# Six edits to a hybrid decoder trunk in split float32: pinned memory scaling, squares on two engines, values out of the bank, weight sums, convolution root, one more tile

## The chip, the cores and the metric

The kernel runs on one core of a Trainium2 chip. The metric is device microseconds (us) of one launch; lower is better. TensorE is PE in all views, VectorE is DVE, ScalarE is ACT, GpSimd is POOL, and SP is the queue that issues most loads. Each engine works off its own instructions in order; engines wait for each other by semaphores.

## The reference

One layer (`DEPTH` 1) on x of 1024 x 1024, in float32. All products have K of 1024. Cut to what matters here:

```python
h = rms_norm(x, norm_g[l])
z = jnp.einsum('bsd,de->bse', h, w_in[l])          # 11 blocks of 1024 columns
u = jax.nn.gelu(z[..., OFF_A_U:OFF_A_U + W])
v = layer_norm(jax.nn.gelu(z[..., OFF_A_V:OFF_A_V + W]), gmlp_ln_g[l], gmlp_ln_b[l])
br_a = gmlp_spatial_gate(u, v, w_s[l], b_s[l]) * jax.nn.silu(z[..., OFF_A_G:OFF_A_G + W])
glu = z[..., OFF_B_A:OFF_B_A + W] * jax.nn.sigmoid(z[..., OFF_B_B:OFF_B_B + W])
c = causal_depthwise_conv(glu, conv_w[l], conv_b[l])            # 31 taps
c = jax.nn.silu(layer_norm(c, conv_ln_g[l], conv_ln_b[l]))
br_b = c * jax.nn.silu(z[..., OFF_B_G:OFF_B_G + W])
mem_n = rms_norm(mem, mem_norm_g[l])                            # 256 x 1024
att = memory_cross_attention(z[..., OFF_C_Q:OFF_C_Q + W], mem_n, w_kv[l])
br_c = att * jax.nn.silu(z[..., OFF_C_G:OFF_C_G + W])
proj = jnp.einsum('bsnw,nwd->bsnd', branches, w_branch[l])
merged = jnp.einsum('bsnd,bsnd->bsd', gates, proj)              # sigmoid gates out of z
x = x + jnp.einsum('bsd,de->bse', merged, w_out[l])
return rms_norm(x, final_norm_g)
```

## The kernel before

Every float32 operand is split into a high part (a cast to fp32r on ACT, L74, or a scaled copy) and a low part (the difference, on DVE, L75); a product is then three matmuls, high x high, high x low and low x high. Where the names end in `hi` and `lo`, or a tile has a leading index 0 and 1, these are the two parts. The large products use seven block products in place of eight; the sums of blocks are formed on DVE for x (`combine`) and, for two of the weights, on the way through DRAM.

The program runs in this order, with the times of the profiled execution:

- **K projection**, 0 to 39 us. `mem_gain(k)` (L210, L211) scales the memory's columns into `mhi`/`mlo`, eight K steps of 128x256 out of two loads `mraw`. Two groups `g` of four weight tiles `kraw`, each of two K steps; a tile goes through `wchunk` (cast `whi`, difference `wlo`), the first one in two halves; L269 does the matmuls. After the fourth tile come the squares of `mtok` (the memory by rows, L135, with a row sum) and `mean_rsqrt` (L99 to L109) for the norm; `diagonals` (L121) puts the result on the diagonal of tiles `dg`, and `spread` (L130, L132) multiplies them with ones, which gives the norm along the other axis.
- **V projection**, 39 to 63 us (L332). Beside it ACT squares the tiles `xtok` (x by rows, eight loads, three of them ahead, `NRAW`) by `squares(n)` into the columns of `xss`. A finished bank is scaled into `vt` (L345) and split from there into `vv`.
- **v of the gMLP**, 66 to 155 us (L380), 16 chunks of 24 matmuls. Behind the first chunk the program does `squares(3)`, `mean_rsqrt` and `diagonals` for x, and behind the second the spread into `rb`, which `x_norm` (L299) multiplies into x.
- **40 half pairs**, 156 to 950 us (L425): the other blocks of `w_in`, some 19 us each. Beside the matmuls DVE forms sums of weight tiles (`sum`, split into `op`), ACT copies one of the banks away (`u`, L462 and L469, for which PE's next block product waits), and DVE does the convolution's 31 taps in pieces (L523). Also here, by a generator `wsum`, the sums of tiles of the branch and output weights: a base load on SP (L629), up to three accumulating DMAs on POOL (L627), a cast `wsh` on ACT and the difference on DVE; both parts are stored later by `flush`. `spump(n)` takes n steps of the list of generators, `spump(1)` ahead of a half pair and `spump(SPUMP)` behind it.
- **Attention and merge**, 951 to 1190 us (L732, L770, L806). `conv_rstd` (L863) makes the reciprocal root of the convolution's mean square: `csq` holds squares, summed over channels tile by tile; a product with `onesd` (L845) sums over partitions, so that each of 128 partitions holds the same 1024 values, and the root is worked out on 128x1024 in two halves. `normed` (L882) multiplies it in. In this stage each bank leaves by `gate` (L739) on DVE.
- **Output product**, 1190 to 1344 us (L938): seven block products again, whose sums of blocks are `sums4` on DVE and whose parts are cast and subtracted as `op`.

The order on each engine follows a scheduler that starts from the program's order; it may move an instruction ahead of others on its engine where nothing depends on it. `keep(...)` around an instruction holds it in the written order.

Of the kernel before, what the change touches and what calls it, by code (L numbers as in the profile page):

```python
# [39 lines left out]
def trunk(ctx, tc, xt, x, memt, wf, wv, wkf, wkv, mem, wbr, wb1, wo, wst, bs, cols, fng, out):  # L40
# [92 lines left out]

    def square(src, dst):
        A.activation(out=src, in_=src, func=AF.Square, accum_out=dst)  # L135

# [29 lines left out]
    def c1(base, k):  # L166
        return col[:, base + k:base + k + 1]
# [40 lines left out]
    def mem_gain(k):  # L208
        src = mraw[k // 4][:, k % 4, :]
        A.activation(out=mhi[k], in_=src, func=AF.Copy, scale=c1(COL_MEMN, k))  # L210
        V.scalar_tensor_tensor(out=mlo[k], in0=src, scalar=c1(COL_MEMN, k), in1=f(mhi[k]),  # L211
                               op0=ALU.mult, op1=ALU.subtract)

# [35 lines left out]
    for g in range(2):  # L249
        pst = [bank() for _ in range(4)]  # L250
        for j in range(4):
            i = 4 * g + j
            if i == 0:
                hi, lo = op((P, 1024), "whi"), op((P, 1024), "wlo")
                for kk2 in range(2):
                    v = slice(kk2 * H, (kk2 + 1) * H)
                    split(kraw[0][:, v], hi[:, v], lo[:, v])
                    mem_gain(kk2)
            else:
                hi, lo = wchunk(None, kraw[i])  # L260
                if g == 0:
                    mem_gain(2 * j)
                    mem_gain(2 * j + 1)
# [47 lines left out]
    def squares(n):  # L311
        for _ in range(n):
            t = min(xtok)
            square(xtok.pop(t), xss[:, t:t + 1])
            if t + NRAW < TT:
                xt_load(t + NRAW)

    for hf in range(2):
        pst = [bank() for _ in range(MT)]
        for c in range(4):  # L320
# [16 lines left out]
            if i == 1:  # L337
                for t in range(NRAW):
# [28 lines left out]
    for th in range(2):  # L367
        va = [slot(s="va") for _ in range(4)]
        for ch in range(2):
            pst = [bank() for _ in range(4)]  # L370
            for c in range(4):
# [249 lines left out]

    def wsum(w, i, j):
        t = slot(F32R, s="ws")
        for n, b in enumerate((SUMB, SUMO)[w][i]):
            src = (wb1, wo)[w][b + j]
            if n:
                G.dma_start(out=f(t), in_=src, accum_op=ALU.add)  # L627
            else:
                nc.sync.dma_start(out=f(t), in_=src)  # L629
                flush()  # L630
            yield
        hi = slot(F32R, s="wsh")
        split(f(t), hi, t)
        unstored.extend(((sdram[w, i, j][0], f(hi)), (sdram[w, i, j][1], f(t))))
        yield

    sums = [wsum(w, i, j) for w in range(2) for i in SUMB for j in range(2)]

    def spump(n):
        while n and sums:  # L640
            try:
                next(sums[0])
                n -= 1
            except StopIteration:
                sums.pop(0)
                if not sums:
                    flush()

# [213 lines left out]
    def conv_rstd():  # L862
        nonlocal crs  # L863
        ps = flat(tokmean(wchunk(None, csq)))
        a, s, y = slot(s="ca"), slot(s="cs"), slot(s="crb")
        for hf in range(2):
            v = slice(hf * H, (hf + 1) * H)
            V.tensor_scalar(a[:, v], ps[:, v], LN_EPS, None, ALU.add)
            A.activation(out=s[:, v], in_=a[:, v], func=AF.Sqrt)
            V.reciprocal(out=y[:, v], in_=s[:, v])  # L870
            V.tensor_tensor(s[:, v], y[:, v], y[:, v], ALU.mult)
            V.tensor_tensor(s[:, v], s[:, v], a[:, v], ALU.mult)
            V.tensor_scalar(s[:, v], s[:, v], -0.5, 1.5, ALU.mult, ALU.add)
            V.tensor_tensor(y[:, v], y[:, v], s[:, v], ALU.mult)
        crs = y

# [10 lines left out]
    for d in range(KT):  # L887
# [200 lines left out]
    s1 = [slot(shape=(P, 2, H), s="s1") for _ in range(2)]  # L1088
    s1 = [s1[k // 2][:, k % 2, :] for k in range(4)]
    sums4(s1, a21, a22)  # L1090
# [20 lines left out]
    oprod(px, o, w, False)  # L1111
    sums4(a12, a12, a11, ALU.add)
    o, w = [gop(v) for v in a12], wn
# [11 lines left out]

SPUMP = 2
NVA = 2
# [11 lines left out]
PUMPA = 8  # L1139
NWARM = 10  # L1140
PUMP = (6, 4, 6, 3, 6, 8, 6, 6, 5, 7)

# [56 lines left out]
```

## Time and profile before

| | |
|---|---|
| runs, us | 1349.16, 1350.61, 1353.12; median 1350.61 |
| profiled execution, us | 1355.2, span 1353.5, mean granted clock 0.987 |
| busy, us | PE 1309.0, DVE 1101.8, ACT 610.9, POOL 117.2 |

A launch's time is a little longer than the span between the first and last instruction of its profile. "Busy" counts time in which an engine executes; weight loads of PE lie beside its matmuls. Idle time of an engine matters only where another one, in the end PE, waits for it.

### The profile page before, as it was taken

The page shows a single profiled execution, that of the slowest core. Times are in us where ns is not written, and L with a number is a line of the kernel's source. Part 1 is how long each engine was busy: PE and PEld are TensorE (multiplying, and loading weights), DVE is VectorE, ACT ScalarE, POOL GpSimd, SP SyncE. Part 2 cuts the span into 40 slices and gives each one's busy share as a digit, 9 for nine tenths or more (in the row PEclk, how much of TensorE's full clock was granted, in tenths as well). Part 3 has the DMA queues.
Part 4 walks back from the last instruction along what each step waited for, and adds up shares of the span by engine and source line. Part 5 has one row for each costly group of instructions (what it writes and reads, how often), then busy time and mean ns, then how long its engine had stood idle before and what let it go on. Part 6 is the DMA issues. An engine that isn't in the chain of part 4 may idle for free.

```text
span 1353.5 us, 16391 instructions
## 1 busy us (share of the span) xinstructions
PE 1309.0 (97%) x6006; PEld 1089.7 (81%) x6006; DVE 1101.8 (81%) x1479; ACT 610.9 (45%) x1017; POOL 117.2 (9%) x203
## 2 busy tenths in 40 slices
PE   7899999999899999999999999999999999799997
PEld 7788888888688788778888888888888888688785
DVE  4788768998885997998899898698599478984776
ACT  5856655344344444344344444344544453322235
POOL 0100011111110111110210000001000010000000
PEclk8999999999899999999999999999999999899998
DMA  9844366766666657556864313335744453656943
GB/s 368 349 141 156 119 232 186 209 205 194 226 194 148 250 193 242 187 173 197 229 217 171 102 63 109 124 141 203 259 169 133 171 218 109 246 189 239 406 177 125
DMA packets 84465, 262.86 MB, mean 194 GB/s; under 512 B 8608, under 2 KB 18336, under 8 KB 84384
## 3 DMA queue, kind: packets, MB, share of 16 engines
q1 hardware_dynamic: 56704, 161.83, 34.1%
q0 software_dynamic: 27392, 99.63, 22.7%
q8 instruction: 47, 0.77, 0.2%
q10 hardware_dynamic: 288, 0.35, 0.1%
q14 instruction: 34, 0.28, 0.1%
HBM read 185.23 MB, written 76.55 MB: 193 GB/s over the span
## 4 chain that ended last, share of the span: by engine, by line
PE 78%; DVE 10%; DMA 7%; issue 3%; ACT 2%; SPq 0%; POOL 0%; DVEq 0%; POOLq 0%; ACTq 0%
PE x L425 24%; PE y L425 12%; PE acc L938 11%; PE acc L732 11%; PE b L380 7%; PE z L425 6%; DMA ws<-in_wb 2%; DVE conv L523 2%; PE acc L770 2%; DVE op L75 2%; PE acc L806 2%; DMA ws<-in_wo 2%; DMA raw<-in_wf 1%; PE b L269 1%; PE b L332 1%
## 5 line engine op out<-in xcount | busy, mean ns | idle before, releaser
L425 PE MATMUL x<-T,op 128*128 128x512 f32 x1440 | 349.7, 392 | 8.8 <-ACT u L462 8.8
L425 PEld LDWEIGHTS x<-T,op 128*128 128x128 f32 x1440 | 270.8, 189 | 67.5 <-ACT u L462 11.4
L523 DVE SCALAR_TENSOR_TENSOR conv<-cb,col,conv 128x994 f32<-128x994 f32 (+14 forms) x120 | 151.8, 1265 | 0.6
L74 ACT CAST op<-sum 128x512 fp32r<-128x512 f32 x160 | 99.4, 622 | 104.7 <-PE z L425 40.1
L75 DVE TENSOR_TENSOR op<-sum,op 128x512 fp32r<-128x512 f32 x160 | 108.7, 685 | 18.8 <-ACT op L74 18.6
L425 PE MATMUL x<-B,op 128*128 128x512 f32 x480 | 115.9, 389 | 2.6 <-DVE op L75 2.6
L425 PE MATMUL z<-B,op 128*128 128x512 f32 x480 | 115.9, 390 | 1.0 <-DVE op L75 1.0
L425 PE MATMUL y<-B,op 128*128 128x512 f32 x480 | 115.4, 389 | 0.0
L425 PE MATMUL y<-T,op 128*128 128x512 f32 x480 | 115.3, 389 | 0.0
L523 DVE SCALAR_TENSOR_TENSOR conv<-ca,col,conv 128x994 f32<-128x994 f32 (+14 forms) x90 | 113.6, 1262 | 0.3
L425 PEld LDWEIGHTS x<-B,op 128*128 128x128 f32 x480 | 90.0, 188 | 21.7 <-DVE op L75 3.1
L425 PEld LDWEIGHTS z<-B,op 128*128 128x128 f32 x480 | 89.9, 188 | 20.5 <-DVE op L75 1.9
L425 PEld LDWEIGHTS y<-B,op 128*128 128x128 f32 x480 | 90.1, 188 | 18.7
L425 PEld LDWEIGHTS y<-T,op 128*128 128x128 f32 x480 | 90.1, 188 | 18.7
L74 ACT CAST op<-raw 128x512 fp32r<-128x512 f32 x120 | 74.3, 620 | 60.4 <-PE y L425 58.9
L75 DVE TENSOR_TENSOR op<-raw,op 128x512 fp32r<-128x512 f32 x120 | 81.9, 684 | 18.6 <-ACT op L74 18.4
L732 PE MATMUL acc<-bhi,wlo 128*128 128x512 f32 x256 | 80.3, 395 | 7.5 <-DVE wlo L75 7.5
L732 PE MATMUL acc<-bhi,whi 128*128 128x512 f32 x256 | 80.4, 396 | 0.9 <-DVE ca L481 0.9
L732 PE MATMUL acc<-blo,whi 128*128 128x512 f32 x256 | 79.6, 392 | 0.0
L938 PE MATMUL acc<-q,sw 128*128 128x512 f32 x288 | 65.4, 389 | 0.0
L938 PEld LDWEIGHTS acc<-q,sw 128*128 128x128 f32 x288 | 54.1, 188 | 11.2
L732 PEld LDWEIGHTS acc<-bhi,wlo 128*128 128x128 f32 x256 | 48.5, 190 | 18.0 <-DVE wlo L75 7.9
(260 smaller groups left out, 2158.4 us busy)
## 6 DMA issues: line engine op xcount, KB each, us to landing
raw<-in_wf SPq DMA_DIRECT2D x80, 512.0 KB, 3.7
sw<-sw SPq DMA_DIRECT2D x56, 512.0 KB, 8.3
sw<-wsh POOLq DMA_DIRECT2D x28, 512.0 KB, 3.5
sw<-ws POOLq DMA_DIRECT2D x28, 512.0 KB, 3.8
raw<-in_wv SPq DMA_DIRECT2D x16, 512.0 KB, 3.6
raw<-in_wbr SPq DMA_DIRECT2D x16, 512.0 KB, 6.3
gate<-g SPq DMA_DIRECT2D x16, 512.0 KB, 4.3
ws<-in_wb SPq DMA_DIRECT2D x14, 512.0 KB, 5.2
```

The costliest lines, as they stand in the source:

```text
L74: A.copy(hi, src)
L75: V.tensor_tensor(lo, src, f(hi), ALU.subtract)
L269: T.matmul(pst[e][:, :M], w[:, ks], m[k], start=(k == 0 and n == 0), stop=(k == KT - 1 and n == 2))
L332: T.matmul(pst[m], a[k][:, ms], w[:, ws], start=(k == 0 and j == 0), stop=(k == KT - 1 and j == 2))
L380: T.matmul(pst[t], q[:, a, ts_], w[:, ws], start=(k == 0 and j == 0), stop=(k == KT - 1 and j == 2))
L425: T.matmul(ps, w[:, a, ks], m[k][:, b, :], start=(start and k == 0 and j == 0), stop=(stop and k == 3 and j == 2), skip_group_check=not start)
L523: V.scalar_tensor_tensor(out=a[:, PAD - j:], in0=g[:, :n], scalar=col[:, cw + j:cw + j + 1], in1=a[:, PAD - j:], op0=ALU.mult, op1=ALU.add)
L732: T.matmul(ps[:, hf, :], w[:, ks], m[k][:, hf * H:(hf + 1) * H], start=(k == 0 and j == 0), stop=(k == KT - 1 and j == 2))
L770: T.matmul(ps[:, i, :], q[a][:, d, i * P:(i + 1) * P], kk[:, b, d, :], start=(d == 0 and j == 0), stop=(d == 1 and j == 2))
L806: T.matmul(ps[:, d, :], vv[:, a, m, d * P:(d + 1) * P], p2[b][:, m, :], start=(m == 0 and j == 0), stop=(m == MT - 1 and j == 2))
L938: T.matmul(ps[t][:, v], a[k][i][:, ts_], w[k][n][:, v], start=(start and k == 0 and j == 0), stop=(k == 3 and j == 2), skip_group_check=no ...
```

## The change

- **Start.** `mem_gain` and the casts of the first four K weight tiles (`ksplit`) are pinned to the written order.
- **Squares.** Odd `xtok` tiles are squared on DVE, as a SCALAR_TENSOR_TENSOR with a row sum; two are done in the V projection instead of five, and six behind the first chunk of v. Four `xtok` loads go ahead (`NXT`).
- **Values.** The V projection's banks go straight into `vv`, scaled on ACT; DVE takes the low part out of the bank. `vt` is gone.
- **Weight sums.** One generator `wsums` for all units: the first load of the next unit is issued ahead of the split of the present one, and each accumulate is a step. `SPUMP` is 1, so a half pair takes two steps.
- **Convolution root.** Eight float32 matmuls with one column of `ones` give the sums with tokens on partitions, 128x8; `mean_rsqrt`, `diagonals` and `spread` (behind the next merge product) make the rest.
- **Output product.** One sum goes into tiles of its own (`s2`), and the sum into `a21` is formed later.

```diff
+def square(src, dst, vector=False):
+    if vector:
+        V.scalar_tensor_tensor(out=src, in0=src, scalar=1.0, in1=src, op0=ALU.mult, op1=ALU.mult, accum_out=dst)
...
-        A.activation(out=mhi[k], in_=src, func=AF.Copy, scale=c1(COL_MEMN, k))
...
+        keep(A.activation(out=mhi[k], in_=src, func=AF.Copy, scale=c1(COL_MEMN, k)))
...
+    def ksplit(src, hi, lo):
+        keep(A.copy(hi, src))
+        keep(V.tensor_tensor(lo, src, f(hi), ALU.subtract))
...
-            square(xtok.pop(t), xss[:, t:t + 1])
+            square(xtok.pop(t), xss[:, t:t + 1], t % 2)
...
-            if i >= 3:
+            if i in (5, 6):
                 squares(1)
...
-            tmp = half("vt")
-            A.activation(out=tmp, in_=pst[m], func=AF.Copy, scale=mr[:, m:m + 1])
...
-                split(tmp[:, hs], vv[hh][:, 0, m, :], vv[hh][:, 1, m, :])
+                A.activation(out=vv[hh][:, 0, m, :], in_=pst[m][:, hs], func=AF.Copy, scale=mr[:, m:m + 1])
+                V.scalar_tensor_tensor(out=vv[hh][:, 1, m, :], in0=pst[m][:, hs], scalar=mr[:, m:m + 1],
+                                       in1=f(vv[hh][:, 0, m, :]), op0=ALU.mult, op1=ALU.subtract)
...
-                        squares(3)
+                        squares(6)
...
+        first(units[0])
+        yield
+        for u, after in zip(units, units[1:] + [None]):
+            w, i, j = u
+            t = tiles.pop(u)
+            for b in (SUMB, SUMO)[w][i][1:]:
+                G.dma_start(out=f(t), in_=(wb1, wo)[w][b + j], accum_op=ALU.add)
+                yield
+            if after:
+                first(after)
+            flush()
+            hi = slot(F32R, s="wsh")
+            split(f(t), hi, t)
...
-        ps = flat(tokmean(wchunk(None, csq)))
...
+        ps = misc()
+        for i in range(TT):
+            T.matmul(ps[:, i:i + 1], csq[:, i * P:(i + 1) * P], ones[:, 0:1], start=True, stop=True)
+        crs = diagonals(mean_rsqrt(ps[:, :TT], TT, LN_EPS), TT)
...
-            crb = crs
+            crb = slot(s="crb")
+            spread(crs, crb, misc)
...
-    sums4(a21, a11, a21)
-    sums4(a11, s1, a11)
+    sums4(s2, s1, a11)
...
-    o, w = [gop(v) for v in a11], wn
+    o, w = [gop(v) for v in s2], wn
+    sums4(a21, a11, a21)
...
-SPUMP = 2
+SPUMP = 1
```

What that does to the order on the engines is shown at three places. ACT at the start, first before, then with the change (`kvraw` are the K weight tiles, `mraw` the memory by columns, `mtok` by rows):

```order
L74 CAST whi_139<-kvraw_85 128x512 x2
L74 CAST whi_176<-kvraw_86 128x1024
L74 CAST whi_211<-kvraw_87 128x1024
L210 ACTIVATE mhi_120<-mraw_83,col 128x256 x4
L135 ACTIVATE mtok_102,mss<-mtok_102 128x1024
L135 ACTIVATE mtok_103,mss<-mtok_103 128x1024
L99 ACT_TABLE_LOAD
L99 ACTIVATE rs_s_284<-ms_282 128x2
L74 CAST whi_246<-kvraw_88 128x1024
L74 CAST rh_293<-rs_y_285 128x2
L210 ACTIVATE mhi_121<-mraw_84,col 128x256 x4
```

```order
L218 CAST whi_139<-kvraw_85 128x512
L213 ACTIVATE mhi_120<-mraw_83,col 128x256
L218 CAST whi_139<-kvraw_85 128x512
L213 ACTIVATE mhi_120<-mraw_83,col 128x256
L218 CAST whi_176<-kvraw_86 128x1024
L213 ACTIVATE mhi_120<-mraw_83,col 128x256 x2
L218 CAST whi_211<-kvraw_87 128x1024
L138 ACTIVATE mtok_102,mss<-mtok_102 128x1024
L138 ACTIVATE mtok_103,mss<-mtok_103 128x1024
L213 ACTIVATE mhi_121<-mraw_84,col 128x256 x2
L218 CAST whi_246<-kvraw_88 128x1024
L213 ACTIVATE mhi_121<-mraw_84,col 128x256 x2
```

The first `mhi` moved from behind three tiles' casts to behind the first half tile's, and the squares of `mtok` now stand between two casts and the second group of `mhi`, without the table load and a cast ahead of that group.

PE at the second chunk of v, before and with the change (`dg` are the diagonals of x's row norms, `xg` the scaled x):

```order
L380 MATMUL b_703<-whi_760,xg_410 128x512 x2
L380 MATMUL b_703<-wlo_761,xg_410 128x512
L380 MATMUL b_703<-whi_760,xg_455 128x512 x2
L380 MATMUL b_703<-wlo_761,xg_455 128x512
L130 MATMUL b_789<-dg_752,onesr 128x512 x2
L130 MATMUL b_793<-dg_755,onesr 128x512 x2
L380 MATMUL b_700<-whi_803,xg_476 128x512 x2
```

```order
L390 MATMUL b_688<-whi_691,xg_336 128x512 x2
L390 MATMUL b_688<-wlo_692,xg_336 128x512
L390 MATMUL b_688<-whi_691,xg_375 128x512 x2
L390 MATMUL b_688<-wlo_692,xg_375 128x512
L130 MATMUL b_781<-dg_744,onesr 128x512 x2
L130 MATMUL b_785<-dg_747,onesr 128x512
L390 MATMUL b_685<-whi_752,xg_410 128x512 x2
```

Before, the four spread matmuls stand behind the second chunk (`whi_760`); now three of them stand behind the first (`whi_691`), the fourth behind the second.

POOL in the half pairs, before and with the change (`ws_2772` and `ws_2921` before are the units that are `ws_2617` and `ws_2767` with the change; `in_wb` rows are accumulates, `g` and `q` stores of half pairs):

```order
L146 DMA q_1518<-ca_2521 128x1024
L146 DMA sw_1541<-ws_2622 128x1024
L627 DMA ws_2772<-in_wb 128x1024
L146 DMA g_285_1471<-cb_2672 128x1024
L146 DMA sw_1542<-wsh_2777 128x1024
L146 DMA sw_1543<-ws_2772 128x1024
L146 DMA g_284_1470<-ca_2671 128x1024
L627 DMA ws_2921<-in_wb 128x1024
L146 DMA g_301_1487<-cb_2822 128x1024
L146 DMA sw_1544<-wsh_2926 128x1024
```

```order
L149 DMA q_1511<-cb_2516 128x1024
L647 DMA ws_2617<-in_wb 128x1024
L149 DMA q_1510<-ca_2515 128x1024
L149 DMA sw_1534<-wsh_2771 128x1024
L647 DMA ws_2767<-in_wb 128x1024
L149 DMA g_281_1463<-cb_2666 128x1024
L149 DMA sw_1535<-ws_2617 128x1024
L149 DMA g_280_1462<-ca_2665 128x1024
L149 DMA sw_1536<-wsh_2920 128x1024
```

The accumulate of `ws_2921` stood behind both stores of the unit before and the second store of its half pair; with the change (`ws_2767`) it stands ahead of the unit's second store and of both stores of that half pair.

## Rows read from the trace of the kernel before

**Rows 1.** The page's busy times: engine, us, share of the span, instructions.
```profile
PE 1309.0 (97%) x6006; PEld 1089.7 (81%) x6006; DVE 1101.8 (81%) x1479; ACT 610.9 (45%) x1017; POOL 117.2 (9%) x203
```

**Rows 2.** What PE waited for: line, releaser, us in total, times, longest.
```profile
PE x L425 <- ACT u L462: 8.8, 5, 5.4
PE acc L732 <- DVE wlo L75: 7.5, 1, 7.5
PE b L269 <- ACT mhi L210: 6.9, 1, 6.9
PE b L380 <- ACT whi L74: 2.9, 1, 2.9
PE x L425 <- DVE op L75: 2.6, 1, 2.6
PE b L332 <- ACT whi L74: 1.1, 1, 1.1
...
PE acc L938 <- DVE op L75: 0.8, 1, 0.8
```

**Rows 3.** Stretches: length, busy PE, PEld, DVE, ACT, POOL (instructions), PEclk, DMA share, GB/s.
```profile
65.00:70.00 5.00, 4.12 (x11) 3.29 (x12) 3.89 (x12) 3.24 (x6) 1.05 (x2) 0.66 0.69 229
...
350.00:355.00 5.00, 5.00 (x18) 3.92 (x18) 5.00 (x7) 1.19 (x3) 0.00 (x0) 0.73 0.26 106
...
1175.00:1180.00 5.00, 2.07 (x5) 1.70 (x6) 5.00 (x5) 2.30 (x2) 0.00 (x0) 0.53 1.02 401
...
1180.00:1185.00 5.00, 5.00 (x19) 4.02 (x18) 5.00 (x8) 3.33 (x5) 0.00 (x0) 0.78 0.88 358
```

**Rows 4.** Timeline, PE and ACT, first 22 us: start, us, instruction [rest before, releaser].
```profile
12.13 0.80 PE L269 MATMUL b<-mhi,whi 128*128 128x256 f32 x2 [6.92 <-ACT mhi L210]
...
11.57 1.70 ACT L210 ACTIVATE mhi<-mraw,col 128x256 fp32r<-128x256 f32 x4
...
15.13 1.06 ACT L135 ACTIVATE mtok<-mtok 128x1024 f32<-128x1024 f32 x1 [1.86 <-DMA mtok<-in_mem]
...
20.20 1.70 ACT L210 ACTIVATE mhi<-mraw,col 128x256 fp32r<-128x256 f32 x4
```

**Rows 5.** Timeline, ACT, DVE and PE, 64 to 79 us.
```profile
64.79 1.04 ACT L74 CAST whi<-raw 128x1024 fp32r<-128x1024 f32 x1
...
67.01 0.16 DVE L109 TENSOR_SCALAR ms<-xss 128x8 f32<-128x8 f32 x1
...
70.61 0.68 DVE L121 TENSOR_TENSOR dg<-ident,rl 128x512 fp32r<-128x512 f32 x1
...
78.52 1.09 PE L130 MATMUL b<-dg,onesr 128*128 128x512 f32 x4
```

**Rows 6.** Timeline, DVE, 1145 to 1177 us (convolution root).
```profile
1145.11 6.57 DVE L870 RECIPROCAL crb<-cs 128x512 f32<-128x512 f32 x2 [0.37 <-ACT cs L869]
...
1155.81 1.21 DVE L739 TENSOR_TENSOR gate<-acc,gate 128x1024 f32<-128x1024 f32 x1
...
1156.94 1.27 DVE L882 SCALAR_TENSOR_TENSOR cm<-cm,col,crb 128x1024 f32<-128x1024 f32 x1
...
1176.66 1.21 DVE L75 TENSOR_TENSOR wlo<-raw,whi 128x1024 fp32r<-128x1024 f32 x1
```

**Rows 7.** Timeline, POOL and ACT, 336 to 345 us, and two waits of ACT.
```profile
336.59 0.88 POOL L627 DMA_DIRECT2D ws<-in_wb  x1 [11.94 <-DMA ws<-in_wb]
...
344.57 1.04 ACT L74 CAST wsh<-ws 128x1024 fp32r<-128x1024 f32 x1 [8.32 <-DMA ws<-in_wb]
...
ACT wsh L74 <- DMA ws<-in_wb: 23.9, 6, 8.3
...
ACT wsh L74 <- DMA ws<-in_wo: 21.4, 6, 5.4
```

**Rows 8.** The stretch 250 to 750 us, columns as in rows 3.
```profile
250.00:750.00 500.00, 487.55 (x2166) 402.10 (x2165) 434.92 (x550) 216.45 (x345) 71.55 (x115) 0.99 0.64 204
```

**Rows 9.** Instructions of L601: ns min/median/max, first and last start.
```profile
L601 PE MATMUL sp<-ws,va x128: 270/275/275, 238.1 to 841.4; 128*128 128x128 f32 x128
```

More of the change, by code (lines that the diff above doesn't have):

```diff
@@ L132, in spread @@
             A.copy(dst[:, i0 * P:(i0 + w) * P], ps[:, :w * P])
-    def square(src, dst):
-        A.activation(out=src, in_=src, func=AF.Square, accum_out=dst)
+    def square(src, dst, vector=False):
+        if vector:
+            V.scalar_tensor_tensor(out=src, in0=src, scalar=1.0, in1=src, op0=ALU.mult, op1=ALU.mult, accum_out=dst)
+        else:
+            A.activation(out=src, in_=src, func=AF.Square, accum_out=dst)
     def sumsq(src, acc_tile, first, w):
@@ L209, in mem_gain @@
         src = mraw[k // 4][:, k % 4, :]
-        A.activation(out=mhi[k], in_=src, func=AF.Copy, scale=c1(COL_MEMN, k))
-        V.scalar_tensor_tensor(out=mlo[k], in0=src, scalar=c1(COL_MEMN, k), in1=f(mhi[k]),
-                               op0=ALU.mult, op1=ALU.subtract)
+        keep(A.activation(out=mhi[k], in_=src, func=AF.Copy, scale=c1(COL_MEMN, k)))
+        keep(V.scalar_tensor_tensor(out=mlo[k], in0=src, scalar=c1(COL_MEMN, k), in1=f(mhi[k]),
+                                    op0=ALU.mult, op1=ALU.subtract))
+    def ksplit(src, hi, lo):
+        keep(A.copy(hi, src))
+        keep(V.tensor_tensor(lo, src, f(hi), ALU.subtract))
     mrb = const.tile([P, M], F32, name="mrb")
@@ L256, in trunk @@
                     v = slice(kk2 * H, (kk2 + 1) * H)
-                    split(kraw[0][:, v], hi[:, v], lo[:, v])
+                    ksplit(kraw[0][:, v], hi[:, v], lo[:, v])
                     mem_gain(kk2)
-            else:
-                hi, lo = wchunk(None, kraw[i])
+            elif g:
+                hi, lo = wchunk(None, kraw[i])
+            else:
+                hi, lo = op((P, 1024), "whi"), op((P, 1024), "wlo")
+                ksplit(kraw[i], hi, lo)
                 if g == 0:
@@ L313, in squares @@
             t = min(xtok)
-            square(xtok.pop(t), xss[:, t:t + 1])
-            if t + NRAW < TT:
-                xt_load(t + NRAW)
+            square(xtok.pop(t), xss[:, t:t + 1], t % 2)
+            if t + NXT < TT:
+                xt_load(t + NXT)
     for hf in range(2):
@@ L337, in trunk @@
             if i == 1:
-                for t in range(NRAW):
+                for t in range(NXT):
                     xt_load(t)
-            if i >= 3:
+            if i in (5, 6):
                 squares(1)
@@ L620, in flush, with wsums, first @@
             store(*unstored.pop(0))
[L622 to L630, printed above, removed]
-            yield
[L632 to L637, printed above, removed]
+    def wsums():
+        units = [(w, i, j) for w in range(2) for i in SUMB for j in range(2)]
+        tiles = {}
+        def first(u):
+            w, i, j = u
+            tiles[u] = slot(F32R, s="ws")
+            nc.sync.dma_start(out=f(tiles[u]), in_=(wb1, wo)[w][(SUMB, SUMO)[w][i][0] + j])
+        first(units[0])
+        yield
+        for u, after in zip(units, units[1:] + [None]):
+            w, i, j = u
+            t = tiles.pop(u)
[7 more added lines that the diff above has]
+            split(f(t), hi, t)
+            unstored.extend(((sdram[w, i, j][0], f(hi)), (sdram[w, i, j][1], f(t))))
+            yield
+        flush()
+    sums = [wsums()]
     def spump(n):
@@ L645, in spump @@
                 sums.pop(0)
-                if not sums:
-                    flush()
     bhi, blo = [None] * KT, [None] * KT
@@ L863, in conv_rstd @@
         nonlocal crs
-        ps = flat(tokmean(wchunk(None, csq)))
[L865 to L875, printed above, removed]
+        ps = misc()
+        for i in range(TT):
+            T.matmul(ps[:, i:i + 1], csq[:, i * P:(i + 1) * P], ones[:, 0:1], start=True, stop=True)
+        crs = diagonals(mean_rsqrt(ps[:, :TT], TT, LN_EPS), TT)
     def center(e):
@@ L1089, in trunk @@
     s1 = [s1[k // 2][:, k % 2, :] for k in range(4)]
+    s2 = [slot(shape=(P, 2, H), s="s2") for _ in range(2)]
+    s2 = [s2[k // 2][:, k % 2, :] for k in range(4)]
     sums4(s1, a21, a22)
-    sums4(a21, a11, a21)
-    sums4(a11, s1, a11)
+    sums4(s2, s1, a11)
     yadd(0, 0, px)
     oprod(py, o, w, True)
-    o, w = [gop(v) for v in a11], wn
+    o, w = [gop(v) for v in s2], wn
+    sums4(a21, a11, a21)
     wn = swload(1, "5", False)
@@ L1111, in trunk @@
     oprod(px, o, w, False)
-    sums4(a12, a12, a11, ALU.add)
+    sums4(a12, a12, s2, ALU.add)
     o, w = [gop(v) for v in a12], wn
@@ L1140 @@
 NWARM = 10
+NXT = 4
 PUMP = (6, 4, 6, 3, 6, 8, 6, 6, 5, 7)
```

## Prediction, before the changed kernel was run

> **What bounds the kernel now.** The busy table comes first: TensorE (PE) is busy 97% of the span [rows 1], so time can come only out of PE's own work or out of its 44.5 us of rest. The change leaves the large products alone; the second view is therefore the list of what PE waited for [rows 2]. Its seven rows are 30.6 us; the rest is the tail behind the last matmul and pieces of a microsecond that the change doesn't touch. The third view is the table of 5 us stretches with the granted clock [rows 3]. Behind PE's longer rests it is a mixture of 1.2 and 2.4 GHz, the chip's two levels; in most other stretches it is 1.00. A stall so costs more than its length: in a stretch in which PE is busy throughout, a clock c loses (1 - c) x 5 us on top. Each of the seven waits lies at a place that the change edits, so the question is how much of each goes, and what is late next.
>
> **Part A, the start (K and V projections, first products of v).** Before, ACT casts all the weight tiles of the first four K steps and only then makes `mhi`; PE has rested 6.92 us when it starts at 12.13 [rows 4]. The change pins `mhi` behind the first cast, so that PE can begin 5 to 7 us earlier, as the first tiles land. But it also puts the `mtok` squares, which wait for data until 15.13, ahead of `mhi` of K steps 5 to 8: two of 1.06 end at 17.5, so step 5 starts near 18, against 21 to 22 behind the `mhi` of 20.20 [rows 4]. Until then PE works in pieces, in part at the lower clock. K ends 0 (all given back there) to 3.6 us earlier; I take 1.5.
> PE's 1.1 in the V projection [rows 2] is a cast behind squares on ACT. Four of the eight go to DVE, and a copy and two casts per bank become two scaled copies of about 0.45, as `mhi` is (four in 1.70 [rows 4]): 1.1 goes. The first product of v waited 2.9 [rows 2] for the cast at 64.79 [rows 5], which stood behind those copies; its load also goes two places up on SP's queue, past two `xtok` loads, and those are wanted later. I take 2.8, and 1.5 of the 1.7 that the clock of 0.66 costs in 65:70 [rows 3].
> Against it, the matmuls that spread the row norms come after 24 products instead of 48. Their `dg` needs the chain from `ms` at 67.01 to the last `dg`, 70.61 + 0.68, so 4.3 us [rows 5], and that starts behind the last square, now on DVE behind the v subtractions, some 2.8 us past V's end (four subtractions and one square). PE gets there 24 x 0.23 = 5.5 us past it (four matmuls 0.23 apart last 1.09 [rows 5]), the chain after 7.1: a new wait of 1.6. In sum 1.5 + 1.1 + 2.8 + 1.5 - 1.6 = **5.3 us** (3 to 8). A square on DVE has no row; the nearest is the same form on two float32 tensors of that shape, 1.27, beside 1.21 for a plain product [rows 6], and I take 1.3.
> The Trainium skill ("Vector Engine (DVE) Microarchitecture Reference", "7. Points that are easy to get wrong") says that this form halves its throughput when both sources lie in SBUF and aren't bf16. Read as a doubled square it would make the new wait 1.3 us longer and part A 4.0; the 1.27 against 1.21 shows no such loss here.
>
> **Part B, the weight sums.** A sum of weight tiles is a base load on SP, accumulating DMAs on POOL and a cast on ACT, as steps of a generator. In the longest case POOL rested 11.94 us for the base, accumulated from 336.59, and ACT sat 8.32 us until that had landed at 344.57 [rows 7]; the `u` copy that PE wanted stood behind the cast, and PE rested 5.4 [rows 2]. ACT waited so 12 times, 45.3 us [rows 7], and 8.8 of it reached PE by `u` [rows 2]. The change issues a base with the unit before and takes two steps per half pair instead of three; on POOL's order the accumulate then stands about a pair, 19 us (40 pairs in 155 to 950), ahead of its cast. Against a landing of 8 that leaves 11. One unit with three accumulates still waits some 2 us, and since 8.32 of ACT's wait cost PE 5.4, ACT has 2.9 to spare. So 8.8 goes, with the clock of 0.73 behind the 5.4, 1.4 [rows 3]: **10.2 us** (5, if half the units meet their DMA again, to 12). On SP's queue the base moves past one or two `raw` loads; they come later by its own transfer and are wanted a pair later, so nothing.
> DVE is next: it is busy 434.92 of 500 us in 250:750 [rows 8], and PE waited 2.6 for an `op` of x [rows 2] behind a `raw` load that accumulates delayed. These now end earlier, which gives 0 to 2.6; I take **1**, because the stalls that go were also DVE's rest.
>
> **Part C, the convolution root.** From DVE go the chain that begins with the reciprocals at 1145.11 (6.57 for two) and ends at 1155.81, 10.7 us, and a split of 1.2 [rows 6]. Added are one chain of eight columns, six steps of about 0.17 (as at 67.01), and four `dg` of 0.68 [rows 5]: 3.7. DVE is 8.2 us lighter ahead of the `wlo` at 1176.66 [rows 6] for which PE rested 7.5 [rows 2]. PE trades four matmuls of 0.23 for four spreads of the same, and gets eight float32 products with one column. No row shows those; float32 128x128 took 0.275 with its load beside it [rows 9], so they cost up to 8 x 0.275 = 2.2, and hardly under 0.9. I take 2.2. The spreads stand 24 matmuls, 5.5 us, behind the sums; the chain is 3.7 and two ACT steps: no wait. But they take two banks for which `gate` then waits, and DVE's `gate` steps wait for PE, so it will not be early by all of the 8.2: I leave 2 of the 7.5. The clock gives 1.1 in 1180:1185 and half of the 2.07 us busy at about 0.5 in 1175:1180, 1.0 [rows 3]. 7.5 + 2.1 - 2 - 2.2 = **5.4 us** (2 to 8).
>
> **Part D, the last products.** `op` of the second product no longer stands behind a sum that only a later one reads; with one `sums4` fewer ahead of it on DVE, the wait of 0.8 [rows 2] goes: **0.7** (0 to 0.8). What is reordered in mean, loads and stores between lies on engines that rest there, beside PE work without a wait: 0.
>
> **Sum.** 5.3 + 10.2 + 1 + 5.4 + 0.7 = 22.6 us. The profiled execution took 1355.2, 4.6 above the median of 1350.6; against its own time this is 1332.6, and for the median **1328 us**. The lower ends sum to 10 and the upper ones to 31.4: 1341 to 1319.
>
> **The rivals.** (1) *DVE becomes the bound of the pairs*: with 13% of rest [rows 8] its `op` splits come late where ACT's casts did, part B keeps 4 and the 1 is lost: 1335. For it speaks the 2.6; against it that most half pairs have no such wait. (2) *The root gives nothing*: another `wlo`, or the bank that `gate` frees late, waits in its place: 1333. (3) *The start gives nothing*: PE starts early and then waits for loads, as ACT does for `mtok` [rows 4], and the early spread eats the rest: 1333. (4) *Slower*: accumulate and cast are now consecutive steps. If POOL comes to the accumulate only in the cast's own half pair, each of the 12 casts that waited takes 8 us, as that of 344.57, and PE 5.4: 65 in place of the 8.8, with the other gains (11.4): 1350.6 + 56 - 11.4 = 1395. It decides once the accumulate lands over 2.9 us behind ACT's readiness. Against it: on POOL's order the next unit's accumulate stands ahead of the store of the one before.
> On that price the Trainium skill ("DMA: Bandwidth & Descriptors", "Anatomy of one DMA — SWDGE (gpsimd) path") gives 2.0 us plus the bytes at 436 GB/s, an estimate of 3.2 us for 512 KB, by which this rival would cost 0.3 x 12 = 4 us and still end faster. The trace's 8 us, beside other loads, decides.
> (5) *The change doesn't do what it says*: `mhi` is pinned but the loads gate PE as before, and casts slide along with their accumulates; only small pieces are left, 1348.
>
> **Numbers.** The forecast gets 0.62, (1) 0.12, (2) and (3) 0.07 each, (4) and (5) 0.06 each. A measurement of this kernel can tell about 0.3%, 4 us, from no change. The first four cases lie below that, 0.88, and a third of (5) with them: faster 0.90, same 0.04, slower 0.06. 1319 to 1341 leaves out (4) and (5), 0.12, and a little at the ends.
>
> **What would show it.** Right: the first K matmul 5 to 7 us earlier; no wait of PE for `u`; ACT no longer resting over 3 us for `ws`; PE's wait for `wlo` at 2 or less; a new wait of 1 to 2 us before the spread matmuls; PE's rest near 25 us in all. Wrong: accumulates that land behind their cast's place; a wait of x or z for `op` above 6; a lower clock in stretches past 75 that were at 1.00.

## The result, and the profile after

The changed kernel takes **1335.14 us** (four runs, 1334.52 to 1336.07) against 1351.31 (four runs, 1349.16 to 1353.12): a ratio of 0.9882, 95% interval 0.9864 to 0.9899, so 16 us faster. The forecast was 1328 with a range of 1319 to 1341. Its profiled execution took 1334.93 with a span of 1333.2.

The changed kernel's page, busy times; they answer to [rows 1]:

```profile
PE 1307.3 (98%) x6022; PEld 1088.5 (82%) x6022; DVE 1095.6 (82%) x1485; ACT 605.5 (45%) x1006; POOL 117.7 (9%) x203
```

PE's work is all but the same (1309.0 before); its rest fell from 44.5 to 25.9 us. What it still waits for, from the list of PE's waits of the changed kernel (columns as in [rows 2]; lines of this kernel behind L132 are 3 to 20 higher, L425 is L435, L732 is L751):

```profile
PE b L279 <- ACT mhi L213: 3.8, 3, 2.9
PE x L435 <- DVE op L75: 2.4, 1, 2.4
PE x L435 <- ACT u L472: 2.3, 2, 1.5
PE acc L751 <- DVE wlo L75: 1.8, 1, 1.8
PE b L130 <- DVE dg L121: 1.3, 2, 1.2
...
PE acc L950 <- DVE op L75: 0.8, 1, 0.8
```

Against [rows 2]: the waits for `u` went from 8.8 to 2.3, for `wlo` from 7.5 to 1.8, for `mhi` from 6.9 to 3.8 in three pieces; those of 2.9 and 1.1 for `whi` are gone; 1.3 ahead of the spread is new; the two for `op` stand. By the first and last matmul of each stage the two profiled executions compare so:

| from | before | after | gained here |
|---|---|---|---|
| start to the first product of the half pairs | 155.6 | 150.3 | 5.3 |
| from there to the first product of the merge | 951.4 | 936.8 | 9.3 |
| from there to the first output product | 1190.0 | 1169.7 | 5.7 |
| from there to the last matmul | 1343.4 | 1323.1 | 0.0 |

The last row holds fourteen block products and not seven: those of the convolution's branch come first, and the output's own seven begin at 1266 before.

Predicted were 5.3, 11.2 (10.2 and 1), 5.4 and 0.7. The profiles differ by 20.3 us, the medians by 16.2.

**The start**, from the timeline of the changed kernel, PE and ACT (start, length, instruction, in brackets the rest before it and what ended it):

```profile
5.52 0.51 PE L279 MATMUL b<-mhi,whi 128*128 128x256 f32 x2 [0.15 <-ACT mhi L213]
...
18.31 0.42 PE L279 MATMUL b<-mhi,whi 128*128 128x256 f32 x1 [2.90 <-ACT mhi L213]
...
15.43 1.06 ACT L138 ACTIVATE mtok<-mtok 128x1024 f32<-128x1024 f32 x1 [3.44 <-DMA mtok<-in_mem]
...
17.77 0.89 ACT L213 ACTIVATE mhi<-mraw,col 128x256 fp32r<-128x256 f32 x2
```

PE begins 6.6 us earlier (12.13 in [rows 4]), works in pieces until 15.4 and then rests 2.9 us until step 5 can start at 18.31, because ACT sat 3.44 us for `mtok` with the scaling of that step queued behind the squares. The last K matmul starts at 37.6 instead of 39.1.

**The first chunks of v**, timeline of DVE and PE in the changed kernel:

```profile
62.95 1.22 DVE L136 SCALAR_TENSOR_TENSOR xtok<-xtok 128x1024 f32<-128x1024 f32 x1
64.09 0.08 DVE L136 DVE_READ_ACCUMULATOR xtok<-xtok 128x1 f32 x1
64.28 0.17 DVE L109 TENSOR_SCALAR ms<-xss 128x8 f32<-128x8 f32 x1
...
67.89 0.68 DVE L121 TENSOR_TENSOR dg<-ident,rl 128x512 fp32r<-128x512 f32 x1
...
66.92 1.01 PE L130 MATMUL b<-dg,onesr 128*128 128x512 f32 x2 [1.15 <-DVE dg L121]
68.12 0.47 PE L130 MATMUL b<-dg,onesr 128*128 128x512 f32 x1 [0.19 <-DVE dg L121]
```

The chain from `ms` to the end of the last `dg` is 4.3 us as before [rows 5], it starts behind the last square on DVE, and PE waits 1.3 in front of it.

**The weight sums**, one sum of the changed kernel in the timeline of POOL and ACT, from the list of ACT's waits the one that is left for a sum's DMA, and that wait in the timeline of SP and ACT:

```profile
306.52 0.91 POOL L647 DMA_DIRECT2D ws<-in_wb  x1 [1.30 <-DMA ws<-in_wb]
...
324.86 0.63 ACT L500 ACTIVATE cb<-cb 128x512 f32<-128x512 f32 x1 [2.37 <-DVE cb L482]
325.40 1.04 ACT L74 CAST wsh<-ws 128x1024 fp32r<-128x1024 f32 x1
```

```profile
ACT wsh L74 <- DMA ws<-in_wb: 4.1, 1, 4.1
```

```profile
342.34 0.86 SPq L639 DMA_DIRECT2D ws<-in_wb  x2
...
349.54 1.05 ACT L74 CAST wsh<-ws 128x1024 fp32r<-128x1024 f32 x1 [4.08 <-DMA ws<-in_wb]
```

This accumulate is issued 18.9 us ahead of its cast (8.0 in the case of [rows 7]), and the cast waits for nothing. Over all sixteen sums that have accumulates, the last one is issued 6.0 to 34.7 us ahead of the cast, with a middle of 16; before it was 5.1 to 19.2, with a middle of 6.5. Of 45.3 us of waits for these DMAs 4.1 are left, at a sum without any accumulate, whose base load SP issues 7 us ahead of the cast.

**The convolution root**, timeline of PE and DVE, and two stretches (columns as in [rows 3]):

```profile
1126.73 1.84 PE L885 MATMUL acc<-ones,csq 128*128 128x1 f32 x16
...
1159.58 0.73 PE L751 MATMUL acc<-bhi,wlo 128*128 128x512 f32 x2 [1.77 <-DVE wlo L75]
...
1158.31 1.22 DVE L75 TENSOR_TENSOR wlo<-raw,whi 128x1024 fp32r<-128x1024 f32 x1
```

```profile
1155.00:1160.00 5.00, 3.23 (x15) 2.37 (x14) 4.64 (x5) 0.00 (x0) 0.00 (x0) 1.00 0.55 205
1160.00:1165.00 5.00, 5.00 (x24) 4.12 (x23) 5.00 (x7) 2.83 (x5) 0.00 (x0) 1.00 0.91 342
```

The eight float32 products take 1.84 us in 16 matmuls; the last weight split is 1.77 late instead of 7.5, and in this execution the clock is at 1.00 behind it, where it was 0.53 and 0.78 [rows 3].

### The profile page after: what moved, and what is told of

Same layout as the page of the kernel before. It is cut to its first block, busy times and chain, and to the rows that moved or that the text cites. A ratio compares the mean times of both kernels' runs of the same rounds, so it can differ in the third digit from the quotient of the medians.

```text
span 1333.2 us, 16422 instructions
## 1 busy us (share of the span) xinstructions
PE 1307.3 (98%) x6022; PEld 1088.5 (82%) x6022; DVE 1095.6 (82%) x1485; ACT 605.5 (45%) x1006; POOL 117.7 (9%) x203
## 4 chain that ended last, share of the span: by engine, by line
PE 86%; DVE 8%; DMA 4%; issue 2%; ACT 1%; SPq 0%; DVEq 0%; ACTq 0%
PE x L435 27%; PE y L435 13%; PE acc L751 13%; PE acc L950 11%; PE z L435 7%; PE b L390 6%; DVE conv L533 3%; DMA raw<-in_wf 2%; PE acc L789 2%; PE acc L825 2%; PE b L342 2%; PE b L279 1%; DVE op L75 1%; PE sp L611 1%; DMA mtok<-in_mem 1%
## 5 line engine op out<-in xcount | busy, mean ns | idle before, releaser
L435 PE MATMUL x<-T,op 128*128 128x512 f32 x1440 | 348.1, 390 | 2.5 <-ACT u L472 2.3
L435 PEld LDWEIGHTS x<-T,op 128*128 128x128 f32 x1440 | 269.6, 188 | 60.4 <-ACT u L472 4.8
L435 PE MATMUL x<-B,op 128*128 128x512 f32 x480 | 116.2, 390 | 2.4 <-DVE op L75 2.4
L435 PE MATMUL z<-B,op 128*128 128x512 f32 x480 | 116.1, 389 | 0.2 <-DVE op L75 0.2
L435 PE MATMUL y<-B,op 128*128 128x512 f32 x480 | 115.4, 389 | 0.0
L435 PE MATMUL y<-T,op 128*128 128x512 f32 x480 | 115.3, 389 | 0.0
L435 PEld LDWEIGHTS x<-B,op 128*128 128x128 f32 x480 | 89.9, 188 | 21.9 <-DVE op L75 3.2
L435 PEld LDWEIGHTS z<-B,op 128*128 128x128 f32 x480 | 90.0, 188 | 19.3 <-DVE op L75 0.6
L435 PEld LDWEIGHTS y<-B,op 128*128 128x128 f32 x480 | 90.1, 188 | 18.7
L435 PEld LDWEIGHTS y<-T,op 128*128 128x128 f32 x480 | 90.1, 188 | 18.7
L751 PE MATMUL acc<-bhi,wlo 128*128 128x512 f32 x256 | 79.3, 390 | 1.8 <-DVE wlo L75 1.8
L751 PE MATMUL acc<-bhi,whi 128*128 128x512 f32 x256 | 79.9, 393 | 0.9 <-DVE ca L491 0.9
L751 PE MATMUL acc<-blo,whi 128*128 128x512 f32 x256 | 79.2, 390 | 0.0
L950 PEld LDWEIGHTS acc<-q,sw 128*128 128x128 f32 x288 | 54.1, 188 | 11.2
L447 DVE TENSOR_TENSOR sum<-raw 128x512 f32<-128x512 f32 x40 | 27.5, 688 | 39.3 <-DMA raw<-in_wf 39.3
```

Source lines behind the costliest of these rows:

```text
L435: T.matmul(ps, w[:, a, ks], m[k][:, b, :], start=(start and k == 0 and j == 0), stop=(stop and k == 3 and j == 2), skip_group_check=not start)
L447: V.tensor_tensor(s1, a21, a22, ALU.add)
L751: T.matmul(ps[:, hf, :], w[:, ks], m[k][:, hf * H:(hf + 1) * H], start=(k == 0 and j == 0), stop=(k == KT - 1 and j == 2))
L950: T.matmul(ps[t][:, v], a[k][i][:, ts_], w[k][n][:, v], start=(start and k == 0 and j == 0), stop=(k == 3 and j == 2), skip_group_check=no ...
```

## Experiments

Times are medians; the kernel before had 1350.9, 1350.3 and 1352.0 in the three sets of runs. "After" is 1335.1; it was timed only in a set ahead of these, with 1351.3 for the kernel before, so a difference from it is one between sets.

### The kernel before once more

> The kernel before, unchanged, profiled a second time. Its first profile took 1355.2 us where its runs have a median of 1351.3. Theory: the 4 us more lie in the waits of PE for the copy u behind a weight sum's cast (8.8 us in the first profile, the longest 5.4), which hang on when an accumulating DMA lands; in a run near the median they are 3 to 5 us shorter in all, and the start, the V projection (wait of 1.1), the first product of v (2.9) and the convolution root (7.5) repeat within 0.5 us each. Rival: the 4 us lie in the start or the root, or are spread over the clock; then u keeps about 8.8.

No edit. It took 1355.27 us. PE's waits:

```profile
PE x L425 <- ACT u L462: 10.0, 5, 5.1
PE acc L732 <- DVE wlo L75: 7.5, 1, 7.5
PE b L269 <- ACT mhi L210: 7.1, 1, 7.1
...
PE x L425 <- DVE op L75: 0.8, 1, 0.8
```

The theory fell: the second profile repeats the first one's time and its waits, `u` rather more. One wait did not repeat: that for `op` of x, 2.6 in the first profile, is 0.8. Of the 43 times of this kernel without a profile, in all sets of runs, three lie above 1355.2 (the highest 1358.3, the lowest 1344.4). So both profiled executions are from the upper end of a kernel whose 43 times spread over 14 us. The changed kernel's four spread over 1.6, but so few can't show a spread: the first four of the kernel before spread over 4.0.

### The old weight sums in the changed kernel

```diff
-    sums = [wsums()]
+    sums = [wsum(w, i, j) for w in range(2) for i in SUMB for j in range(2)]
...
-SPUMP = 1
+SPUMP = 2
```

(with `wsum` as before)

> The changed kernel with the weight sums as before (one generator for a unit, three steps a half pair); the rest stays changed. Theory: the sums gave 9.3 us between the two profiles (half pairs 791.8 us long before, 782.5 after), but 4 of them were a bad draw of the first profile; so 1335.1 + 5.3 = 1340.4 us, between 1339 and 1342, and PE's waits for u between 4 and 6 us. Rival 1: all 9.3 are the sums' in every run: 1344.4. Rival 2: the sums matter little and the half pairs got shorter because the stages ahead shifted: under 1337.

1340.56 us (six runs, 1335.8 to 1344.9; ratio to before 0.9926, 0.9903 to 0.995): 5.4 more than after, as the theory has it, and in its profile the half pairs take 791.5 us against 786.5. PE's wait for `u` is 7.1, above the theory's 4 to 6. In the profile PE waits for `u` and ACT for the sums' DMAs again:

```profile
PE x L435 <- ACT u L472: 7.1, 4, 5.2
...
ACT wsh L74 <- DMA ws<-in_wb: 24.4, 7, 8.1
ACT wsh L74 <- DMA ws<-in_wo: 20.9, 6, 4.9
```

The six times spread over 9 us. That the time is uneven because a wait hangs on when a DMA lands is a guess: no two profiles show it with different landings.

### The new weight sums alone

The kernel before with `wsums` and `SPUMP = 1`.

> The kernel before with the new weight sums alone. Theory: the same 5.4 us that undoing them cost: before's 1350.6 goes to 1345 us (1343.5 to 1346.5), with at most 3 us of PE's waits for u left. Rival 1: 9 to 10 us, as the two profiles have it for the half pairs: 1341. Rival 2: the new sums need the earlier end of the start, and give 2 us or less alone: 1348.5 or above.

1344.43 us (twelve runs, 1342.6 to 1347.2; before 1351.95 in the same set; ratio 0.9944, 0.9926 to 0.9963): the time lies in the theory's range; against before in the same set it is 7.5 us gained, between the theory's 5.4 and rival 1's 9 to 10. Its twelve times spread over 4.6 us, the seventeen of the kernel before beside them over 13.8. No wait for `u` is in its list of PE's waits; ACT's waits for the sums' DMAs and a larger wait for `op` are:

```profile
PE x L425 <- DVE op L75: 4.0, 2, 2.8
...
ACT wsh L74 <- DMA ws<-in_wb: 2.9, 2, 2.4
```

So the new sums don't need the earlier start, and what they give is in part taken by DVE.

### The old convolution root, twice

```diff
-            crb = slot(s="crb")
-            spread(crs, crb, misc)
+            crb = crs
```

(with `conv_rstd` as before)

> The changed kernel with the convolution root as before (split, product with the filled square, root on 128x1024). Theory: the reciprocal chain on DVE makes the last weight split late again: PE's wait for wlo goes from 1.8 to 7 or 8 us with a lower clock behind it; 1335.1 + 5.7 = 1340.8 us (1340 to 1342). Rival: the gain of that stage came from other things (loads, gate order), then under 1337.

1338.70 us (six runs, 1337.3 to 1343.5): 3.6 more than after, less than the 5.7 expected. The profiled execution, 1343.28, shows the expected wait in full in its list of PE's waits, and the lower clock in the two stretches around its end (columns as in [rows 3]):

```profile
PE acc L751 <- DVE wlo L75: 7.5, 1, 7.5
```

```profile
1160.00:1165.00 5.00, 0.00 (x0) 0.00 (x0) 5.00 (x5) 1.99 (x2) 0.00 (x0) 0.57 1.00 379
1165.00:1170.00 5.00, 4.69 (x11) 3.72 (x12) 5.00 (x7) 1.55 (x3) 0.00 (x0) 0.50 1.03 418
```

Its stage from the merge to the output took 239.5 us against 232.9, so 6.6 more.

> The kernel with the old convolution root once more, for a second profile: its six times fell into two groups, 1337.3 to 1338.8 and 1343.3 to 1343.5, and the first profile is of the upper one, with PE's wait for wlo of 7.5 us and a clock of 0.50 to 0.57 in the 10 us around it. Theory: the groups differ by whether the lower clock follows that wait; a run of the lower group has the same 7.5 us of wait and 1.00 or nearly so behind it. Rival: the wait itself is shorter in the lower group (3 us or so), or the difference lies in the half pairs. If this run is of the upper group again, nothing is told.

1341.43 us, between the two groups. The wait is 7.5 again and the stage 239.4 us:

```profile
1160.00:1165.00 5.00, 1.48 (x4) 1.19 (x5) 5.00 (x5) 2.30 (x2) 0.00 (x0) 0.50 1.00 385
1165.00:1170.00 5.00, 5.00 (x15) 3.96 (x14) 5.00 (x7) 2.79 (x5) 0.00 (x0) 0.60 0.99 404
```

So both profiles have the root's full price of 6.5 us in its own stage, and four of the five times without a profile are only 2 to 4 us above after. Whether in those the clock stayed up, the wait was shorter, or something else ran quicker, no profile shows. The mean granted clock of each run bears on it: 0.989 in both of the upper group, 0.990 to 0.993 in the four of the lower. That is 0.001 to 0.004 of 1340 us, an estimate of 1 to 5 us, so the clock carries a part of the difference; how much stays open.

### The start: everything back, and each edit back

```diff
-        keep(A.activation(out=mhi[k], in_=src, func=AF.Copy, scale=c1(COL_MEMN, k)))
+        A.activation(out=mhi[k], in_=src, func=AF.Copy, scale=c1(COL_MEMN, k))
...
-        keep(A.copy(hi, src))
-        keep(V.tensor_tensor(lo, src, f(hi), ALU.subtract))
+        split(src, hi, lo)
```

> The changed kernel with the scaling of the memory and the first casts not pinned, as before. Theory: PE starts near 12 us instead of 5.5, but what it does until 18 in the pinned order is only 24 matmuls beside waits; the V projection ends 1.9 us later (3.0 of shift in the profiles less the wait of 1.1 that the values and squares took): 1337.0 us (1336 to 1338). Rival 1: the early start is given back wholly, because the loads set when K ends: 1335. Rival 2: the pins carry the start, 3 us or more: 1338 or above.

1335.96 us (five runs, 1334.8 to 1338.4): 0.8 more than after, between rival 1's 1335 and the theory's 1336. PE starts at 12.4; K ends 1.8 later, the half pairs begin 3.5 later (153.8), and they end 1.2 later.

```diff
-            square(xtok.pop(t), xss[:, t:t + 1], t % 2)
+            square(xtok.pop(t), xss[:, t:t + 1])
...
-            if i in (5, 6):
+            if i >= 3:
```

(with `squares(3)` and `NXT = 3`)

> The changed kernel with all squares of x on ACT, three loads ahead and five squares in the V projection, as before; pins and values stay changed. The spread matmuls then stand behind 48 products again. Theory: PE's wait of 1.1 in the V projection returns, the first product of v waits about 1 more, the new wait of 1.3 ahead of the spread goes: the half pairs begin 0.5 to 1.5 us later and the time is 1335.1 to 1336.5. Rival: squares on ACT delay the values' copies, and the first product of v waits 2.5 or more: 1337.5 or above.

1336.66 us (six runs, 1334.0 to 1339.0), 1.5 more, just above the theory's range. In its profile the half pairs begin 4.2 us later than in after's (154.5), where the theory had 0.5 to 1.5. The wait in the V projection did not return; the first product of v waited longer than it had before:

```profile
PE b L390 <- ACT whi L74: 3.5, 1, 3.5
```

The third kernel has the values copied to `vt` and split from there, as before.

> The changed kernel with the values copied to vt and split from there, as before; pins and squares stay changed. Theory: a copy and two casts per bank instead of two copies put about 1 us more on ACT ahead of the last square and the x norm's chain, so that the wait ahead of the spread grows from 1.3 to 2 to 3 us: 1336 us (1335.3 to 1337). Rival: the bank is freed earlier by one copy, and nothing or less than nothing is lost: 1335 or below.

1336.32 us (six runs, 1334.9 to 1339.2), 1.2 more, in the theory's range, but by another mechanism: the wait ahead of the spread falls to 0.3, and the V projection waits instead:

```profile
PE b L342 <- ACT whi L74: 2.5, 1, 2.5
```

> The changed kernel with the whole start as before: no pins, all squares on ACT at the old places, values over vt. In the two profiles the start ended 5.3 us earlier with the change (half pairs begin at 150.3 instead of 155.6). Theory after the run without pins, where the half pairs began 3.5 us later and ended only 1.2 later: a part of what the start gains is given back in the half pairs, whose DVE and loads set a part of their pace; this gives 1335.1 + 3 = 1338 us (1337 to 1339.5). Rival: all 5.4 stay: 1340.5.

1339.32 us (six runs, 1335.8 to 1340.9): 4.2 more, less than the 5.3 of the two profiles. Its own profile, 1340.89, keeps all of it: the half pairs begin at 155.8 and take 787.1 us. The three singly cost 0.8, 1.5 and 1.2, none of them more than the resolution found below, and their half pairs begin 3.5, 4.2 and 1.7 us later, which doesn't add up to the 5.5 of all together; how the start's gain divides among them is not shown. In all profiles with the new sums the half pairs take 783.4 to 787.5 us, wherever they begin; this spread of 4 us is as large as the effects, so how much of the start they give back can't be told from one profile of each.

### The last products' sums as before

```diff
-    sums4(s2, s1, a11)
+    sums4(a21, a11, a21)
+    sums4(a11, s1, a11)
```

> The changed kernel with the sums of the last products as before. The prediction had 0.7 us for them; the profile of the changed kernel still has a wait of 0.76 for op in the output product, now read as one at the first product, whose op comes out of the gate and stands behind no sum. Theory: 1335.1 us, within 0.5, and the same wait of 0.8. Rival: 1335.8, with a second wait at the second or third product.

1333.59 us (six runs, 1332.2 to 1335.0), 1.5 less than after, outside what either theory has. But the output stage takes 153.5 us in it and 153.4 in the changed kernel, with the same single wait:

```profile
PE acc L950 <- DVE op L75: 0.8, 1, 0.8
```

In the profiles the difference lies in the half pairs, 783.5 us against 786.5, which the edit doesn't reach. So no gain of the edit is seen, and differences of 1.5 us between variants in different sets of runs can't be taken for effects.

### Squares of the memory behind the scaling

```diff
-                    square(mtok[t], mss[:, t:t + 1])
+                    keep(square(mtok[t], mss[:, t:t + 1]))
```

> The changed kernel with one more pin: the squares of mtok stand on ACT behind the scaling of K steps 5 to 8 instead of ahead of it. In the changed kernel PE rests 2.9 us at 18.3 for that scaling, after 1 to 2 us of pieces, and runs at the lower clock until about 22. Theory: the weight tile of steps 7 and 8 lands near 14, so that K goes on from about 13 to 14; K ends 3 us earlier, half pairs begin 2 to 3 us earlier, the time is 1333 us (1332 to 1334.5) if half of it survives the half pairs. Rival 1: the loads of the start, at 410 GB/s from 10 to 60 us, gate the second half of K or the V projection, and nothing is left: 1335. Rival 2: all survives: 1332 or below.

1332.60 us (four runs, 1331.3 to 1335.3; ratio to before 0.987, 0.9851 to 0.9889): the best of the measured kernels, but its interval overlaps that of after, and the profiled execution took 1335.3. In the profile K ends 2.8 us earlier (34.8) and the V projection ends where it did (59.5); PE's rest moved to places where ACT waits for the weights of V:

```profile
PE b L279 <- ACT whi L74: 2.0, 1, 2.0
PE b L342 <- ACT whi L74: 1.9, 1, 1.9
...
ACT whi L74 <- DMA kvraw<-in_wkv: 5.4, 4, 2.4
```

So under the profile rival 1 holds: the loads set when V ends. That execution is also the slowest of the four, and its stage from the merge to the output took 1.5 us more than after's (234.4): behind the same wait of 1.8 for `wlo` the clock fell here. What the other three gained is not seen.

```profile
1160.00:1165.00 5.00, 5.00 (x18) 4.05 (x17) 4.16 (x6) 3.33 (x5) 0.00 (x0) 0.73 0.97 381
```

### And the spread behind the second chunk

```diff
-                        spread(xdg, rb, bank)
+                        spread(xdg, rb, bank, True)
```

(`True` puts `keep` around its matmuls; on top of the kernel above)

> The changed kernel with the mtok squares pinned behind the scaling of K steps 5 to 8, and with the spread of x's row norms pinned behind the second chunk of v, where it stood before. The first alone gave 1332.6 (one profiled run 1335.3, in which the loads of the V projection's weights gave back what K had gained). Theory: the wait of 1.3 to 1.4 ahead of the spread goes too, without a new one, as the spread is needed only by x norm steps on DVE with rest behind it: 1331.3 us (1330 to 1332.5). Rival: the x norms come late by 5 us and are wanted by the products of the second half or the combines: nothing is gained over 1332.6, or up to 1 us lost.

1336.28 us (six runs, 1334.1 to 1337.7): nothing gained, rather 3.7 lost against the kernel above, which was timed in another set. The 1.3 ahead of the spread is gone, and the second chunk itself waits:

```profile
PE b L392 <- DVE wlo L75: 1.8, 1, 1.8
PE b L392 <- ACT whi L74: 1.2, 1, 1.2
```

The chain for the row norms is then still ahead of that chunk's weight split on DVE, so PE waits for the same work under another name.

## Why the prediction was right, and where it was off

- **Start, 5.3 predicted, 5.3 in the profiles.** Every piece came: PE at 5.5; step 5 at 18.3 (18); K 1.5 earlier (1.5); both `whi` waits gone with the lower clock of 65:70 (now 1.00); the new wait ahead of the spread 1.3 (1.6). The square on DVE takes 1.22 and 0.08 for its sum, against 1.3 taken, beside 1.22 for a plain product of that shape. The Trainium skill ("Vector Engine (DVE) Microarchitecture Reference", "7. Points that are easy to get wrong") has this form at half its throughput; the trace shows no such loss. Undoing the whole start costs 4.2. The clock term, 1.5, is less sure than it looks: the kernel before with the new sums alone has the old start and its waits, and its clock in 65:70 was 1.00 and not 0.66; its half pairs began at 154.3 and not 155.6:

```profile
65.00:70.00 5.00, 4.11 (x18) 3.42 (x19) 3.89 (x12) 3.25 (x6) 1.05 (x2) 1.00 0.70 224
```

- **Weight sums, 10.2 predicted.** The mechanism is shown: ACT's waits fell from 45.3 to 4.1, and PE's waits for `u` are 7.1 to 10.0 us in the three profiles with the old sums, 0 to 3.0 in the eleven with the new. The lead that the text took, 19 us, is that of one sum; the middle is 16 and the shortest 6.0. The wait at a sum with three accumulates did not come, and the one that is left has none. The size was too large by the `u` waits that stay: 2.3 of 8.8. They are no longer behind a DMA; ACT's copy at 357.62 (and one at 377.73) stands behind `ca`, for which ACT waited 4 us each on DVE:

```profile
356.66 1.06 ACT L498 ACTIVATE ca<-ca 128x1024 f32<-128x1024 f32 x1 [4.02 <-DVE ca L491]
357.62 0.57 ACT L472 COPY u<-x 128x512 f32<-128x512 f32 x1
```

  The half pairs got 9.3 shorter between the two profiles. In times, undoing the sums costs 5.4, and alone they give 7.5.
- **DVE, 1 predicted.** This step failed. PE's wait for `op` went from 2.6 to 2.4, but at another half pair. Timeline of DVE and PE in the changed kernel:

```profile
479.28 0.69 DVE L447 TENSOR_TENSOR sum<-raw 128x512 f32<-128x512 f32 x1 [3.49 <-DMA raw<-in_wf]
...
483.60 2.60 PE L435 MATMUL x<-B,op 128*128 128x512 f32 x10 [2.44 <-DVE op L75]
```

  Before, DVE sat 5.59 us at 434.73 for a `raw` load, and PE rested at 456. That wait was one of that execution: the longest for `op` of x is 0.8 in the second profile of before, and 0.6 where the old sums are put back. The one near 483 belongs to the new sums: a wait of 2.0 to 2.8 stands between 480 and 490 us in all eleven profiles that have them. What delays DVE there is argued and not shown: POOL issued an accumulate at 468.66 and SP the `raw` load at 470.20, but no run takes that accumulate away.
- **Root, 5.4 predicted, 5.7 in the profiles.** The remaining wait for `wlo` is 1.8 (2 taken), the spread needed no wait, and in this execution the clock came back in full. That is not so every time: of the nine profiles with the new root and a wait of 1.8, two have the lower clock behind it (with the old sums, and with the memory's squares behind the scaling), and this stage is some 1.5 us longer in them. The float32 products took 1.84, near the 2.2 taken, by luck: [rows 9] counts 128 matmuls, two for each of 64 products, and 0.275 is the length of one that overlaps the next. Two errors cancel; the row's pace, which the last section shows, gives 1.87 for eight products. In the timed runs undoing the root costs 3.6.
- **Last products, 0.7 predicted, 0.** The step read the wait of 0.8 at the wrong product. The `op` in question is the first of the output's, made from `gate`, and no sum stands ahead of it; DVE and PE before:

```profile
1269.96 0.68 DVE L75 TENSOR_TENSOR op<-gate,op 128x512 fp32r<-128x512 f32 x1
...
1270.70 5.51 PE L938 MATMUL acc<-sw,op 128*128 128x512 f32 x23 [0.76 <-DVE op L75]
```

- **The sum.** Against the profile of before it was 22.6, measured 20.3. The larger miss is the step from the profile to the median: the text subtracted the profile's 4.6 over the median from both kernels. The changed kernel's profile has no such offset (1334.9 against 1335.1); with 1332.6 as the forecast the miss would be 2.5 in place of 7. What makes the offset is not settled. Three things bear on it: the two profiles of before have mean granted clocks of 0.987 and 0.986, where the fastest timed run of that kernel has 0.995, so clock losses that the terms took from one execution are not the same in each; the old sums come with a spread of 9 us when they are put into the changed kernel; and the old root costs 6.5 in its two profiles but 3.6 by the median, which would be 3 of the 4 us.
- **The rivals.** The time itself, 1335, is the one of (1), so it doesn't decide between (1) and the forecast. (1) is there in part: DVE's `ca` and `op` hold 4.7 us of PE's waits, and the sums are worth 5.4 to 7.5 in times, between the 4 of (1) and the 10.2. Against (1) in full stand the 9.3 us by which the half pairs got shorter in the profiles. (4), casts directly behind their accumulates, is refuted: none of the sixteen casts with accumulates waited. (3) holds for what one would add: with K quicker still, loads set V's end under the profile.

## What to carry to other kernels

Give an accumulating DMA a whole work unit of lead and issue its base with the unit before; here the times also spread less with it, 4.6 us over twelve runs against 13.8 over seventeen, which no single profile tells. A sum made on one profile holds for that execution: look at the spread of the times before carrying it to a median, since an offset of the old kernel need not pass to the new one. And give a wait to a part of a change only when the producer of the very tile is found on the late engine: `op` was two different things here.

## What was not expected of the hardware

A float32 product with a single column cost what one with 128 columns costs. Each of the eight became two matmuls with a weight load of 0.19 us each, which overlap, and the 16 took 1.84 us, 0.115 apiece. The spatial products of [rows 9] have 128 columns and took 0.117 apiece; one group of them in the changed kernel, where L601 is L611:

```profile
232.69 3.73 PE L611 MATMUL sp<-ws,va 128*128 128x128 f32 x32
```

So the columns don't set this price. That the weight loads do is likely, but no run varies them.

PE's clock did not follow from the length of a rest alone. Behind 7.5 us of rest it was at 0.53 and 0.78, mixtures of 1.2 and 2.4 GHz. Behind 1.77 us at the same place it stayed at 1.00 in the changed kernel, and fell to 0.73 behind the same wait where the memory's squares stand behind the scaling. A clock loss read from one execution is therefore not a fixed part of a wait's price.
